# A modulation sum moved from VectorE to ScalarE and GpSimd, and one copy of B for the scan states

## The chip, the core and the metric

The kernel runs on one core of a Trainium2 chip. The core has TensorE (matmuls, PE in the profile, with the weight loads as PEld), VectorE (DVE), ScalarE (ACT), GpSimd (POOL) and SyncE (SP), which here only issues the transfers. Each engine executes its own instruction queue in order, and they wait for one another by semaphores. The metric is the device time of one execution in microseconds; the times here are the median of several runs.

## What is computed

Two layers of a diffusion backbone over 512 latent tokens of width 1024, with 256 context tokens. A conditioning vector gives each layer six modulation vectors:

```python
mod = (silu(c) @ ada_w[i] + ada_b[i])[:, None, :]
sh1, sc1, g1, sh2, sc2, g2 = jnp.split(mod, N_MOD, axis=-1)      # parts 0 to 5
hx = modulate(rms_norm(x, norm_mix[i]), sh1, sc1)
# layer 0: attention (8 heads) beside a bidirectional scan, both from one input projection
m_lat, _ = hybrid_mixer(hx, hc, ...)       # layer 1: shortconv_mixer(hx, ...)
x = x + g1 * m_lat
x = x + g2 * swiglu(modulate(rms_norm(x, norm_ffn[i]), sh2, sc2), w_gate, w_up, w_down)
```

The scan works in chunks of 128 tokens: two of context, four latent ones. For each chunk, direction and group it forms a state, a product of B (128 tokens x 64) and the decayed inputs (128 tokens x 256):

```python
states = einsum('bclgn,bgecl,bclgep->bcgepn', bc, decay_to_end, xdt)
h = h * chunk_decay + states        # forward over the chunks, and backward for the other direction
```

## The kernel before

Everything is kept with features on the partitions, in float32. A large matmul is made of three of reduced type: each operand is split into a high part (a cast on ScalarE, L94) and a rest (a subtraction on VectorE, L95), and `mm3` (L114 to L118) adds high x high, high x rest and rest x high. Weights come through one ring of three staging buffers named `wst` (512 KB each, L107) and are split into rings of `whi` and `wlo`, also three each.

Layer 0's mixer (`mixer`, L388) first projects keys, values, queries and six feature tiles. It then runs three Python generators round by round (L497 to L505). `ssd` (L695) makes features 6 to 9, advances the scan's states, and then does eight `ssd_unit`s, one per chunk and group (L740). `attention` (L846) does eight heads in two rounds each, and prepares the row maxima of a later head (`attn_prep`, L787, its maximum on VectorE at L804, its diagonal matrix on ScalarE at L805) while it runs the scores and exponentials of the present one (`attn_head`, L811, exponentials at L824). The third is `ada_rest` (L236).

`ada_rest` computes modulation parts as a weighted sum over the 1024 rows of `ada_w`. Per half part (512 columns) it loads four pieces of 2 x 128 rows into `wst` (L251). The first slice is multiplied by its column of silu(c) on VectorE (L255), and the other seven are multiplied and added there (L257, one operation each, two full operands and a per-partition scalar). A 32x32 block transpose (L260) and a reduction (L261) leave 16 numbers per partition in `red`. When all parts are done, one small matmul (L264) folds the partitions, and L269 adds the bias. In the mixer it is called for layer 0's parts 2, 3 and 4: the gate of the mixer, needed at L916 in the projection that follows, and the shift and scale of the first FFN, needed in `entry` (L937) behind that. Its accumulator and its transposed copy lie in `xtok`, in the two context chunks. It is pumped two steps per round from the seventh round on. The parts of layer 1 and part 5 are summed in the same way during the first FFN, with an accumulator `ada_acc`.

The states: `to_tok` (L578) transposes feature 4, which holds B, and copies it for each chunk to `btok` twice side by side, once for each direction, six copies on ScalarE (L590). `ssd_states` (L645) multiplies the inputs by the decay on GpSimd (L652) and takes the matmul with the doubled B (L656), so its output has 128 partitions, of which the forward direction uses the lower and the backward one the upper 64. For the context both directions come from one matmul of 512 columns per chunk and group. For the latent chunks `advance` (L704) does one direction and chunk after the other, with one matmul of 256 columns per group, each with its own PSUM bank. `ssd_advance` (L663) scales the old state on GpSimd (L673) and adds the new one on VectorE (L676). PSUM has three banks of kind A, one of kind V and two double ones of kind S.

The order of the instructions on each engine isn't the program's: a planner takes, in a modelled run, for each engine the earliest instruction in program order that is ready. An instruction that comes late in the program but has its data early fills gaps. Only where the program says so (`manual_schedule`) an engine keeps the program's order. What the planner wrote is fixed, so an engine waits for an instruction in front although a later one may be ready.

## Time and profile before

| | us |
|---|---|
| median of three runs (1287.85 to 1292.81) | 1289.33 |
| the profiled execution | 1291.26 |
| its span in the trace | 1289.4 |
| TensorE busy | 1239.6 (96%) |
| VectorE busy | 729.4 (57%) |
| ScalarE busy | 448.4 (35%) |
| GpSimd busy | 179.5 (14%) |

The shares are averages over stages with different limits. About 1.9 us of the profiled execution lie around its span. Matmuls are pipelined and their ends are modelled, so busy times of TensorE overlap and a busy TensorE is not one at its peak. The stretch around the change, with the context states, the attention, the scan and the modulation sum, goes from about 130 to 326 us.

### The profile page before, as it was taken

To read this page: it belongs to the slowest core of one execution; us is meant where nothing else is said; L and a number is where in the kernel's file an instruction comes from. 1 tells how busy PE (TensorE), PEld (TensorE's weight loads), DVE (VectorE), ACT (ScalarE), POOL (GpSimd) and SP (SyncE) were. 2 spreads that over 40 slices of the span, in tenths; PEclk is the share of its full clock that TensorE was granted. 3 is DMA by queue.
4 is the path that set the end of the run, shared out by engine and by line. 5 is a ranking of instruction groups with operands and counts; after the bars stand their busy time and mean duration, and the time that the engine had idled before them with its cause. 6 is when DMAs were issued, how large, how long until landed. Compare 5 with 4: busy or idle time off the path is not lost.

```text
span 1289.4 us, 15875 instructions
## 1 busy us (share of the span) xinstructions
PE 1239.6 (96%) x6086; PEld 1021.6 (79%) x6086; DVE 729.4 (57%) x1187; ACT 448.4 (35%) x675; POOL 179.5 (14%) x199
## 2 busy tenths in 40 slices
PE   5998988899999999999999999999999999999997
PEld 3887765567898888888888988888988888888886
DVE  4898799985564777788422554443743333332223
ACT  3534534455353222223222342223532222222221
POOL 3423335440220000000000100002200000000001
PEclk9999989999999999999999999999999999999998
DMA  9331343300514777777333323333133333333322
GB/s 369 127 99 49 96 155 125 115 17 1 163 50 143 227 243 243 235 240 249 118 91 94 111 79 93 95 97 112 50 114 98 99 98 98 97 91 90 94 87 66
DMA packets 54845, 158.52 MB, mean 123 GB/s; under 512 B 6000, under 2 KB 8688, under 8 KB 54512
## 3 DMA queue, kind: packets, MB, share of 16 engines
q1 hardware_dynamic: 54480, 157.20, 38.1%
q8 instruction: 48, 0.79, 0.2%
q10 hardware_dynamic: 288, 0.31, 0.1%
q14 instruction: 29, 0.24, 0.1%
HBM read 154.86 MB, written 2.10 MB: 122 GB/s over the span
## 4 chain that ended last, share of the span: by engine, by line
PE 83%; DVE 9%; DMA 3%; issue 3%; POOL 1%; ACT 0%; SPq 0%; DVEq 0%; ACTq 0%; POOLq 0%
PE psS L116 14%; PE psS L117 14%; PE psS L118 14%; PE psA L116 10%; PE psA L118 10%; PE psA L117 10%; DVE xtok L257 2%; PE psV L830 2%; DMA adaw<-ada 2%; PE psS L961 1%; PE psS L822 1%; DVE mx L804 1%; DVE wlo L95 1%; PE psS L963 1%; DMA xT<-xT 1%
## 5 line engine op out<-in xcount | busy, mean ns | idle before, releaser
L95 DVE TENSOR_TENSOR wlo<-wst,whi 128x1024 fp32r<-128x1024 f32 (+2 forms) x194 | 235.0, 1214 | 315.2 <-ACT whi L94 312.3
L94 ACT CAST whi<-wst 128x1024 fp32r<-128x1024 f32 (+2 forms) x194 | 198.2, 1025 | 544.8 <-PE psS L117 242.1
L116 PE MATMUL psS<-act_hi,whi 128*128 128x512 f32 x760 | 297.0, 391 | 1.2 <-DVE cs_a L573 1.0
L117 PE MATMUL psS<-act_lo,whi 128*128 128x512 f32 x760 | 296.7, 390 | 0.0
L118 PE MATMUL psS<-act_hi,wlo 128*128 128x512 f32 x760 | 296.6, 390 | 0.0
L118 PEld LDWEIGHTS psS<-act_hi,wlo 128*128 128x128 f32 x760 | 143.1, 188 | 29.7
L116 PEld LDWEIGHTS psS<-act_hi,whi 128*128 128x128 f32 x760 | 143.0, 188 | 29.5 <-issue 1.2
L117 PEld LDWEIGHTS psS<-act_lo,whi 128*128 128x128 f32 x760 | 143.0, 188 | 27.9
L325 POOL TENSOR_TENSOR sq_acc<-sq_acc,sq 128x512 f32<-128x512 f32 (+1 forms) x28 | 38.0, 1356 | 872.5 <-issue 645.8
L116 PE MATMUL psA<-ffn_h_hi,whi 128*128 128x512 f32 (+1 forms) x396 | 145.3, 367 | 0.0
L118 PE MATMUL psA<-ffn_h_hi,wlo 128*128 128x512 f32 (+1 forms) x396 | 144.9, 366 | 0.0
L117 PE MATMUL psA<-ffn_h_lo,whi 128*128 128x512 f32 (+1 forms) x396 | 144.8, 366 | 0.0
L257 DVE SCALAR_TENSOR_TENSOR ada_acc<-ada_st,silu_c,ada_acc 128x512 f32<-128x512 f32 x98 | 73.4, 749 | 27.5 <-DMA ada_st<-ada 26.0
L117 PEld LDWEIGHTS psA<-ffn_h_lo,whi 128*128 128x128 f32 x396 | 74.7, 189 | 12.1
L116 PEld LDWEIGHTS psA<-ffn_h_hi,whi 128*128 128x128 f32 x396 | 74.7, 189 | 12.0
L118 PEld LDWEIGHTS psA<-ffn_h_hi,wlo 128*128 128x128 f32 x396 | 74.7, 189 | 12.0
L116 PE MATMUL psA<-act_hi,whi 128*128 128x512 f32 (+1 forms) x216 | 80.0, 370 | 0.0
L118 PE MATMUL psA<-act_hi,wlo 128*128 128x512 f32 (+1 forms) x216 | 79.2, 367 | 0.8 <-DVE wlo L95 0.8
L117 PE MATMUL psA<-act_lo,whi 128*128 128x512 f32 (+1 forms) x216 | 79.5, 368 | 0.0
L916 DVE SCALAR_TENSOR_TENSOR xT<-psA,mod,xT 128x512 f32<-128x512 f32 (+1 forms) x40 | 25.7, 643 | 68.2 <-PE psA L118 68.0
L94 ACT CAST ffn_h_hi<-sg 128x512 fp32r<-128x512 f32 x44 | 27.4, 622 | 59.1 <-DVE sg L980 59.1
L118 PEld LDWEIGHTS psA<-act_hi,wlo 128*128 128x128 f32 x216 | 40.8, 189 | 8.0 <-DVE wlo L95 1.3
(297 smaller groups left out, 1804.4 us busy)
## 6 DMA issues: line engine op xcount, KB each, us to landing
wst<-w_gu SPq DMA_DIRECT2D x88, 512.0 KB, 3.6
ada_st<-ada SPq DMA_DIRECT2D x112, 256.0 KB, 4.0
wst<-w_dn SPq DMA_DIRECT2D x32, 512.0 KB, 3.5
wst<-ada SPq DMA_DIRECT2D x24, 512.0 KB, 3.8
wst<-w_sc SPq DMA_DIRECT2D x24, 512.0 KB, 3.6
adaw<-ada SPq DMA_DIRECT2D x16, 512.0 KB, 10.4
wst<-w_dn SPq DMA_DIRECT2D x16, 384.0 KB, 3.2
wst<-w_f SPq DMA_DIRECT2D x10, 512.0 KB, 3.6
```

The lines of the kernel that those rows point to most:

```text
L94: nc.scalar.copy(hi, src)
L95: nc.vector.tensor_tensor(lo, src, hi.bitcast(F32), ALU.subtract)
L116: nc.tensor.matmul(out, lhsT=a[0], rhs=b[0], start=start, stop=False)
L117: nc.tensor.matmul(out, lhsT=a[0], rhs=b[1], start=False, stop=False)
L118: nc.tensor.matmul(out, lhsT=a[1], rhs=b[0], start=False, stop=stop)
L257: nc.vector.scalar_tensor_tensor(a, w[:, i], c, a, ALU.mult, ALU.add)
L325: nc.gpsimd.tensor_tensor(self.acc[:, ts], self.acc[:, ts], sq, ALU.add)
L804: nc.vector.tensor_reduce(mx[:, c:c + 1], s[:, 0:768], AX.X, ALU.max)
L822: nc.tensor.matmul(s[:, a * T:a * T + T], lhsT=kt[x][:, ks], rhs=q[x], start=(x == 0), stop=(x == 1))
L830: nc.tensor.matmul(av, lhsT=vz[:, kc, vs], rhs=e[:, a], start=(c + a == 0), stop=(c + a == CHUNKS - 1))
L916: nc.vector.scalar_tensor_tensor(xt[:, d, ts], ps, gate[:, d:d + 1], xt[:, d, ts], ALU.mult, ALU.add)
L961: nc.tensor.matmul(out, lhsT=a[:, k * P:(k + 1) * P], rhs=hi, start=(k == 0 and a is w[0]), stop=False)
```

## The change

Three things are changed.

1. The modulation sum of layer 0's mixer is split. Part 2 stays as it was on VectorE, pumped one step per round from the seventh round. Parts 3 and 4 get a generator of their own, pumped one step per round from the second round. It multiplies each slice by its column in place on ScalarE and adds the slices on GpSimd into a new accumulator `ada_more`. Transposes and reductions stay on VectorE, into other columns of `red`; there are now two folds.
2. B is kept once in `btok`: two copies instead of six.
3. `ssd_states` takes pairs of chunk and direction. Each has a matmul of 64 output rows and 256 columns, forward into the lower and backward into the upper 64 partitions of one bank, the two behind each other in fixed order. `advance` makes both states first and then both advances.

```diff
-    def ada_rest(self, pool, layer, parts, acc=None, bufs=2, tag=None):
+    def ada_rest(self, pool, layer, parts, acc=None, bufs=2, tag=None, pair=False, red=0):
...
                         c = self.sc[:, 0, k + i:k + i + 1]
-                        if k + i == 0:
+                        if pair:
+                            nc.scalar.activation(w[:, i], w[:, i], AF.Copy, scale=c)
+                            if k + i:
+                                nc.gpsimd.tensor_tensor(a, w[:, 0] if k + i == 1 else a, w[:, i], ALU.add)
+                        elif k + i == 0:
                             nc.vector.tensor_scalar(a, w[:, i], c, None, ALU.mult)
                         else:
                             nc.vector.scalar_tensor_tensor(a, w[:, i], c, a, ALU.mult, ALU.add)
...
-                nc.vector.tensor_reduce(self.red[:, 2 * n + j], tr.rearrange("p (b i) -> p b i", i=32), AX.X, ALU.add)
+                nc.vector.tensor_reduce(self.red[:, red + 2 * n + j], tr.rearrange("p (b i) -> p b i", i=32), AX.X, ALU.add)
...
-        nc.tensor.matmul(ps, lhsT=self.con("fold"), rhs=self.red[:, 0:2 * np_], start=True, stop=True)
+        nc.tensor.matmul(ps, lhsT=self.con("fold"), rhs=self.red[:, red:red + 2 * np_], start=True, stop=True)
...
-        btok = sm.tile([P, CHUNKS, 2, 2, 64], F32, name="btok")
+        btok = sm.tile([P, CHUNKS, 2, 64], F32, name="btok")
...
-        ada = [self.ada_rest(None, 0, (2, 3, 4), (xtok[:, 0], xtok[:, 1]))]
+        more = mp.tile([P, T], F32, name="ada_more")
+        ada = [self.ada_rest(None, 0, (2,), (xtok[:, 0], xtok[:, 1]))]
+        other = [self.ada_rest(None, 0, (3, 4), (more, xtok[:, 1]), pair=True, red=4)]
...
             alive = (next(a, 1) is None) or alive
+            if rounds > 0:
+                self.pump(1, other)
             if rounds > 5:
-                self.pump(2, ada)
+                self.pump(1, ada)
             rounds += 1
         self.pump(1000, ada)
+        self.pump(1000, other)
...
-            s = tp.rearrange("p c (g n) -> p c g n", g=2)
-            for c in range(nc_):
-                nc.scalar.copy(btok[:, c0 + c], s[:, c, :, None, :].broadcast_to([P, 2, 2, 64]))
+            nc.scalar.copy(btok[:, c0:c0 + nc_], tp.rearrange("p c (g n) -> p c g n", g=2))
...
-    def ssd_states(self, sp, sd, c, dirs, tag):
+    def ssd_states(self, sp, sd, ends, tag):
...
-            st = self.psA()
-            for e in dirs:
+            st = self.psA((P, 256))
+            for c, e in ends:
                 nc.gpsimd.tensor_tensor(
...
-            lo, n = 256 * dirs[0], 256 * len(dirs)
-            nc.tensor.matmul(st[:, lo:lo + n], lhsT=sd["btok"][:, c, g].rearrange("p a b -> p (a b)"),
-                             rhs=xw.rearrange("p a b c -> p (a b c)")[:, lo:lo + n], start=True, stop=True)
-            for e in dirs:
-                r = slice(64 * e, 64 * e + 64)
-                out.append((g, e, st[r, 256 * e:256 * e + 256]))
+            with self.tc.manual_schedule(engines={mybir.EngineType.PE}):
+                for c, e in ends:
+                    nc.tensor.matmul(st[64 * e:64 * e + 64], lhsT=sd["btok"][:, c, g], rhs=xw[:, e], start=True, stop=True)
+                    out.append((g, e, st[64 * e:64 * e + 64]))
...
-        st0 = self.ssd_states(pp, sd, 0, (0, 1), "cs_a512")
+        st0 = self.ssd_states(pp, sd, ((0, 0), (0, 1)), "cs_a512")
...
-        st1 = self.ssd_states(pp, sd, 1, (0, 1), "cs_a512")
+        st1 = self.ssd_states(pp, sd, ((1, 0), (1, 1)), "cs_a512")
...
         def advance(a, b):
+            st = self.ssd_states(sp, sd, ((2 + a, 0), (2 + b, 1)), "da")
             for f, t, e in ((a, a + 1, 0), (b, b - 1, 1)):
-                self.ssd_advance(sd, hin[t], hin[f], self.ssd_states(sp, sd, 2 + f, (e,), "da"), 2 + f, e)
+                self.ssd_advance(sd, hin[t], hin[f], st, 2 + f, e)
```

## Rows read from the trace of the kernel before

**Rows 1.** Stages: us, busy PE, PEld, DVE, ACT, POOL, granted clock, DMA share, GB/s:

```profile
160.00:180.00 20.00, 16.21 (x56) 11.52 (x56) 17.78 (x27) 6.94 (x12) 8.42 (x13) 0.83 0.45 148
220.00:240.00 20.00, 17.19 (x61) 11.10 (x60) 18.51 (x31) 9.12 (x15) 10.48 (x9) 0.91 0.33 103
270.00:290.00 20.00, 18.91 (x76) 12.89 (x75) 15.00 (x28) 10.03 (x16) 8.50 (x8) 1.00 0.00 1
290.00:326.00 36.00, 36.00 (x164) 26.14 (x163) 19.03 (x41) 18.41 (x29) 0.00 (x0) 1.00 0.00 1
150.00:270.00 120.00, 105.24 (x397) 71.78 (x396) 113.36 (x179) 49.69 (x82) 56.84 (x58) 0.96 0.38 119
193.00:284.00 91.00, 80.89 (x300) 52.48 (x299) 83.85 (x139) 43.03 (x72) 47.22 (x40) 0.98 0.30 92
```

**Rows 2.** Waits of TensorE, 150 to 290 us: total us, times, longest:

```profile
PE psS L802 <- DVE mx L804: 3.2, 3, 1.3
PE psS L751 <- DVE mx L804: 2.9, 2, 1.7
PE psS L822 <- DVE mx L804: 2.3, 1, 2.3
PE psS L751 <- ACT ex L824: 2.0, 2, 1.2
PE psA L779 <- DVE lx L774: 1.5, 2, 1.4
PE psA L808 <- ACT dm L805: 1.5, 1, 1.5
PE psA L656 <- DVE zf L479: 0.9, 1, 0.9
```

**Rows 3.** Chain of waits, 186 to 230 us, shares by line:

```profile
by line: DVE xtok L257 23.7%; DVE mx L804 10.9%; PE psV L830 7.8%; PE psS L822 6.5%; issue 6.2%; DVE ada_red L261 4.5%; DVE xtok L255 4.4%; PE psS L802 3.9%; DVE xtok L260 3.3%; DVE lx L774 3.3%; PE psA L758 2.6%; DVE hin L676 2.5%; DVE lx
```

**Rows 4.** VectorE's groups, 150 to 270 us: count, busy us, mean ns, idle before:

```profile
L257 DVE SCALAR_TENSOR_TENSOR xtok<-wst,silu_c,xtok 128x512 f32<-128x512 f32 x42 | 36.3, 865 | 2.7 <-DMA wst<-ada 2.2
...
L255 DVE TENSOR_SCALAR xtok<-wst,silu_c 128x512 f32<-128x512 f32 x6 | 4.9, 824 | 0.9 <-DMA wst<-ada 0.9
L260 DVE STREAM_TRANSPOSE xtok<-xtok 128x512 f32<-128x512 f32 x6 | 4.2, 700 | 0.1
...
L261 DVE TENSOR_REDUCE ada_red<-xtok 128x16 f32<-128x512 f32 x6 | 4.0, 674 | 0.1
```

**Rows 5.** Timeline of VectorE at 313 us: start, us, operation:

```profile
313.04 0.76 DVE L269 TENSOR_TENSOR mod<-psA,vecs 32x24 f32<-32x24 f32 x4 [0.33 <-PE psA L264]
```

**Rows 6.** ScalarE's groups, 750 to 870 us:

```profile
L1026 ACT ACTIVATE sc_a<-sc_g,vecs 128x512 f32<-128x512 f32 x8 | 5.8, 723 | 0.0
```

**Rows 7.** GpSimd's groups, whole span:

```profile
L325 POOL TENSOR_TENSOR sq_acc<-sq_acc,sq 128x512 f32<-128x512 f32 x20 | 30.6, 1532 | 851.8 <-issue 645.8 <-ACT sq L322 205.9
```

**Rows 8.** Timeline of GpSimd at 338 us:

```profile
338.15 3.84 POOL L325 TENSOR_TENSOR sq_acc<-sq_acc,sq 128x512 f32<-128x512 f32 x2 [53.21 <-ACT sq L322]
```

**Rows 9.** Timeline of VectorE at 201 us:

```profile
201.37 2.93 DVE L257 SCALAR_TENSOR_TENSOR xtok<-wst,silu_c,xtok 128x512 f32<-128x512 f32 x2
```

**Rows 10.** Timeline of GpSimd at 201 us:

```profile
201.26 1.04 POOL L755 TENSOR_TENSOR da<-cons,dta_hi 128x512 fp32r<-128x512 f32 x1 [0.96 <-PE psA L758]
202.26 1.49 POOL L755 TENSOR_TENSOR da<-cons,dta_lo 128x512 fp32r<-128x512 f32 x1
203.71 1.48 POOL L770 TENSOR_TENSOR lx<-lx,dt 128x512 f32<-128x512 f32 x1
```

**Rows 11.** The page's group of the same sum in the first FFN:

```profile
L257 DVE SCALAR_TENSOR_TENSOR ada_acc<-ada_st,silu_c,ada_acc 128x512 f32<-128x512 f32 x98 | 73.4, 749 | 27.5 <-DMA ada_st<-ada 26.0
```

**Rows 12.** TensorE's groups, 140 to 326 us, the states:

```profile
L656 PE MATMUL psA<-xw,btok 128*128 128x256 f32 x24 | 7.6, 430 | 0.9 <-DVE zf L479 0.9
...
L656 PE MATMUL psA<-xw,btok 128*128 128x512 f32 x8 | 4.5, 641 | 2.2 <-POOL xw L652 1.1 <-ACT btok L590 1.1
```

**Rows 13.** Timeline of TensorE at 34 us:

```profile
34.37 1.07 PE L203 MATMUL psS<-adaw,silu_w 128*32 128x256 f32 x16 [1.08 <-issue]
```

## The prediction

> **What bounds the kernel now.** I read the stage table first, because the busy shares of the whole span hide the place: the change works between about 130 and 326 us, where the context states, the attention and the scan run. From 290 us on TensorE is busy without a gap (36.00 of 36.00 us), and nothing off TensorE can be worth time there [rows 1]. From 150 to 270 us it is different: VectorE is busy 113.36 of 120.00 us (94.5%), TensorE 105.24, ScalarE 49.69 and GpSimd 56.84 [rows 1]. So TensorE stands idle 14.8 us there, 12.3%. The stretch 270 to 290 us does the same kind of work without the modulation sums on VectorE: VectorE 15.00 of 20.00 us (75%), TensorE idle 1.09 us (5.5%) [rows 1].
>
> Next the waits of TensorE, which say who is late. Of its nine rows between 150 and 290 us the seven longest stand: VectorE ends 3.2 + 2.9 + 2.3 + 1.5 + 0.9 = 10.8 us of them, ScalarE 2.0 + 1.5 = 3.5 us, GpSimd none [rows 2]. Most of VectorE's are the row maximum L804, which frees a score bank of PSUM; it is late because it stands in VectorE's queue behind other work. The chain of waits says which work: from 186 to 230 us L257, L261, L255 and L260, all of the modulation sum, hold 23.7 + 4.5 + 4.4 + 3.3 = 35.9% of the chain, some 15.8 of 44 us [rows 3]. The idle time costs twice: the granted clock is 0.83 in 160 to 180 us and 0.91 in 220 to 240 us, so a part of both stretches ran at 1.2 instead of 2.4 GHz, while TensorE waited for 3.8 of the first 20 us and 2.8 of the second [rows 1]. At full clock that is (1 - 0.83) x 20 + (1 - 0.91) x 20 = 5.2 us.
>
> **What leaves VectorE.** Six half parts cost 42 L257 of 865 ns, 6 L255 of 824, 6 transposes of 700 and 6 reductions of 674 [rows 4]. Parts 3 and 4 are four of the six. Their 28 L257 and 4 L255 go: 28 x 0.865 + 4 x 0.824 = 27.5 us. Their transposes and reductions stay, and a second fold with its four small additions L269 adds about 0.8 us (four of 24 elements took 0.76 us) [rows 5]; the fold's own matmul is of the same small kind. In the rows of before the fold's result came at 313 us, long after the last sum; it has to be there only for the gate of the projection and the entry of the FFN behind it, so I put no price on its time.
>
> **What comes to ScalarE and GpSimd.** 32 products (eight per half part). The same form, Copy with a scale vector, 128x512, takes 723 ns at L1026 [rows 6]: 23.1 us. Then 7 sums per half part, 28 in all, of two full 128x512 operands. The nearest row is the sum of squares L325, 1532 ns on average; two in a row took 3.84 us, 1.92 each [rows 7, 8]. That is 42.9 us, with 53.8 us as the upper end.
>
> **What of it is given back: the collision.** The traces show VectorE and GpSimd slowing each other. At 201.37 us two L257 take 2.93 us together, while GpSimd runs three operations back to back, of which the second and third take 1.49 and 1.48 us after 1.04 for the first [rows 9, 10]. In the first FFN the same L257 averages 749 ns over 98 [rows 11]; taken as its unhindered length, one collision costs VectorE about 0.72 us. If none of the 28 sums meets such an operation it is nothing, if all do, 20 us; I take half, 10.1 us, since two thirds of the operations exposed to it (the L257) leave, while the scan's own stay. VectorE's relief is then 27.5 - 0.8 - 10.1 = 16.6 us, and its load in 150 to 270 us 96.8 of 120, or 81%.
>
> One rule speaks against the change. The Trainium skill (SBUF — State Buffer, section "SBUF: two separate sides") says that the port pair that VectorE and GpSimd share is an exclusive lock, held for a whole instruction, with the loser fully blocked. The trace agrees only in part: three GpSimd operations and two L257 would have needed 3 x 1.04 + 2 x 0.75 = 4.6 us one after the other and took 3.9 [rows 9, 10]. What full blocking would make of the time is the second rival.
>
> **What that is worth on TensorE.** Between 81% load and the two states that I have, 94.5% with 12.3% idle and 75% with 5.5%, a straight line gives 7.6% idle, 9.1 us instead of 14.8: 5.7 us won. The upper end is all that VectorE ends, 10.8 us. I take 8, since the sums are not spread evenly over VectorE's work but sit on the chain [rows 3]. Of the 5.2 us of low clock I take half, 2.6 (ends 0 and 5.2).
>
> **The states.** Before, 12 products of 256 columns and 4 of 512, each in two instructions, took 7.6 + 4.5 = 12.1 us of TensorE's (overlapping) busy time [rows 12]; half of each output was thrown away for the context. Now 20 products of 64 output rows and 256 columns, in pairs that lie in different column halves of the array. The row for such halves is the start's L203: 16 instructions with 32 output rows and 256 columns in 1.07 us [rows 13]. That is 0.067 us each, where a full-width row of 256 columns has 430 ns with overlap [rows 12]. So the pairs gain something between nothing and half, and up to 4 us; I take 2 us on the path, as part of TensorE's time there is covered by waits. Half as many PSUM banks per advance help GpSimd, on which nobody waits. Two copies of B instead of six end the 1.1 us that TensorE waits for it [rows 12]: 0.6 us.
>
> **What the new work costs on the path.** (a) ScalarE goes from 49.7 to about 73 of 120 us, 41% to 61%. Behind a product stand the exponentials L824 and L767 and the diagonal L805, for which TensorE waits. Scaling TensorE's 3.5 us of such waits by the load gives 5.2, so 1.7 us (ends 0 and 5). (b) The wait for the 16 loads of parts 3 and 4 moves from VectorE's queue to ScalarE's. VectorE waited 2.2 + 0.9 = 3.1 us for 24 [rows 4], so 2.1 us, of which half counts: 1.0. Those loads also stand in SyncE's queue ahead of two output weights, which nobody needs before the projection. (c) GpSimd's own queue: behind a sum stand the decay operands L755 and the scaling L770, which feed TensorE and VectorE. Of 28 sums, some nine should fall among the scan's units, and delay an operand by less than their length: 2.0 us (ends 0 and 28 x 1.53 = 43). (d) The four transposes wait for the last sum of a half part, with L804 behind them, and the next half part's first sum waits for the transpose, as there is one accumulator: 1.0 us (ends 0 and four times 1.9). Together 5.7 us.
>
> **The sum.** Gains 8.0 + 2.6 + 2.0 + 0.6 = 13.2, costs 5.7, net 7.5 us. The profiled execution took 1291.26 us, so 1283.8; it lies 1.93 us above the median of the runs, so the forecast is 1281.8 us.
>
> **Rivals.** *The sums hold VectorE* (no change). Every sum meets an operation that reads two operands, and 20.2 us of the 26.7 come back. VectorE's load stays at (113.4 - 6.5) / 120 = 89%, idle time on the line at 10.4%, 2.3 us won, and 2.6 for states and copies; costs 5.7, net +0.8 us: 1290 us. For it: GpSimd gets a long operation per 128x512 slice. Against it: the 42 L257 average 865 ns although GpSimd is busy 57 of 120 us [rows 1, 4], so before only a few collided.
>
> *Every sum blocks VectorE for its whole length* (slower). Where each of the 28 sums stops VectorE for 1.53 us instead of 0.72, 42.9 us come against the 26.7 that leave, and the 16.2 us of difference lengthen a stretch that VectorE already fills: nothing won there, 2.6 for states and copies, costs 5.7, so 1291.3 + 16.2 - 2.6 + 5.7 = 1310.6, on the median 1309 us. Against it: three operations and two L257 took less than their sum [rows 9, 10]. This is what the rule of the Trainium skill named above (SBUF — State Buffer, section "SBUF: two separate sides") would do here if every sum met an exposed operation.
>
> *GpSimd becomes the bound* (slower). From 193 to 284 us the eight units run, 91 us, with 47.2 us of GpSimd [rows 1]. If all sums fell there at 1.92 us, 47.2 + 53.8 = 101 us: 10 us more than there is. The context's gain of 2.6 stays, VectorE's is gone: 1291.3 + 10.0 - 2.6 = 1298.7, on the median 1297 us. It decides from (91 - 47.2) / 1.92 = 23 sums in that stretch. For it: the loads share three buffers with the weights, and are late if these hold them. Against it: the new sums start a round after the first feature, and GpSimd has long idle time before 193 us (8.42 busy of 20 in 160 to 180) [rows 1].
>
> *VectorE was the whole limit* (more gain). All 10.8 us and the full 5.2 of clock come back, states give 4, and the costs hide: 1291.3 - 10.8 - 5.2 - 4 - 0.6 + 2 = 1272.7, on the median 1271 us.
>
> **How the numbers follow.** Forecast 0.50 (1276 to 1287 us), VectorE held 0.24, whole blocking 0.03, GpSimd bound 0.09, whole limit 0.14. The time given is the forecast's. The range 1271 to 1291 us leaves out the two slower cases and about half of the last. A measurement tells about 0.5% from no change: 1282.9 and 1295.8 us. Faster takes all of the last case and 0.38 of the forecast, 0.52; same the rest of the forecast and VectorE held, 0.36; slower the blocking and the GpSimd case, 0.12.
>
> **What would show it.** Right: VectorE in 150 to 270 us falls to about 80%, L257 is x14 there, TensorE's waits for L804 shrink to a third, the granted clock stays above 0.95 in 160 to 180 us, and the units end some 7 us earlier, with the kernel behind 330 us as long as before. Wrong: L773, L774 and L757 rows that grow by GpSimd's length; waits of TensorE for L755; transposes L260 waiting for GpSimd; or an idle time of TensorE that stays although VectorE is free, which would mean that the attention's own chain set the pace.

## The result, and the profile after

The changed kernel takes 1303.7 us (median of four runs, 1301.5 to 1304.8) against 1290.5 us for the kernel before (median of four). The ratio is 1.0097, with a 95% interval from 1.0075 to 1.0118: slower by 13 us, where 7.5 us of gain were forecast. The profiled execution took 1301.5 us, with a span of 1299.7; it is the fastest of the four.

The stages, in the columns of [rows 1]: time, busy PE, PEld, DVE, ACT and POOL with their counts, granted clock, DMA share, GB/s.

```profile
160.00:180.00 20.00, 16.01 (x68) 10.77 (x67) 15.06 (x21) 10.57 (x18) 14.24 (x18) 0.91 0.50 159
220.00:240.00 20.00, 15.18 (x44) 9.78 (x44) 19.63 (x26) 10.56 (x16) 18.60 (x14) 0.83 0.38 113
290.00:326.00 36.00, 34.91 (x164) 25.77 (x165) 27.05 (x59) 22.25 (x36) 1.04 (x2) 1.00 0.00 1
150.00:270.00 120.00, 100.79 (x362) 65.12 (x363) 89.42 (x132) 61.73 (x102) 87.64 (x82) 0.91 0.36 114
193.00:284.00 91.00, 78.36 (x273) 50.09 (x273) 73.13 (x115) 47.79 (x78) 60.99 (x49) 0.93 0.28 88
```

From 150 to 270 us VectorE fell from 113.36 to 89.42 us, to 75% (forecast 81%). TensorE did not gain by it: it is idle 19.2 us instead of 14.8, and its granted clock fell from 0.96 to 0.91. GpSimd rose from 56.84 to 87.64 us. From 220 to 240 us VectorE is still busy 19.63 of 20 us, and the clock is 0.83 there.

TensorE's waits between 150 and 290 us, in the columns of [rows 2] (L829, L786, L815, L809 were L822, L779, L808, L802; the maximum L811 was L804):

```profile
PE psS L829 <- DVE mx L811: 4.5, 4, 2.4
PE psA L786 <- DVE lx L781: 3.7, 2, 2.9
PE psA L815 <- ACT dm L812: 3.3, 1, 3.3
PE psS L809 <- DVE mx L811: 2.9, 1, 2.9
```

The waits for the row maximum, 3.2 + 2.9 + 2.3 = 8.4 us before, are 4.5 + 2.9 = 7.4; a third was forecast. The wait for L781, the last step of the scan's decay matrix on VectorE, went from 1.5 to 3.7 us.

The groups of the new work on ScalarE and GpSimd, and of the scan's multiply-add on VectorE, from 150 to 270 us: count, busy us, mean ns, idle time before with its cause.

```profile
L255 ACT ACTIVATE wst<-wst,silu_c 128x512 f32<-128x512 f32 x28 | 18.8, 715 | 16.9 <-DMA wst<-ada 15.3 <-issue 1.7
L257 POOL TENSOR_TENSOR ada_more<-ada_more,wst 128x512 f32<-128x512 f32 x23 | 32.8, 1426 | 5.3 <-ACT wst L255 2.8 <-issue 1.6
L780 DVE SCALAR_TENSOR_TENSOR lx<-lx,dt 128x128 f32<-128x128 f32 x20 | 10.7, 593 | 0.0
```

The multiply-add in the kernel before, in the same stretch:

```profile
L773 DVE SCALAR_TENSOR_TENSOR lx<-lx,dt 128x128 f32<-128x128 f32 x24 | 8.4, 408 | 0.0
```

Product and sum cost what was forecast (715 ns for 723, 1426 for 1532). What was not forecast is the multiply-add, 593 ns instead of 408; the prediction named its growth (L773) as a sign of being wrong. Four L780 in a row take 1.13 us where GpSimd leaves them alone (at 245.71 us in this trace); that is 0.28 us each. Here is one such group with what follows it, and GpSimd beside it (start, length, instruction, count):

```profile
230.49 4.60 DVE L780 SCALAR_TENSOR_TENSOR lx<-lx,dt 128x128 f32<-128x128 f32 x4
235.01 0.68 DVE L894 TENSOR_TENSOR ao<-ao,as 128x512 f32<-128x512 f32 x1
235.61 0.68 DVE L781 TENSOR_TENSOR lx<-lx,cbs 128x512 f32<-128x512 f32 x1
236.21 2.06 DVE L95 TENSOR_TENSOR wlo<-wst,whi 128x1024 fp32r<-128x1024 f32 x1
238.19 1.76 DVE L95 TENSOR_TENSOR act_lo<-ao,act_hi 128x512 fp32r<-128x512 f32 x1
239.87 0.94 DVE L811 TENSOR_REDUCE mx<-psS 128x1 f32<-128x768 f32 x1
```

```profile
227.06 4.44 POOL L257 TENSOR_TENSOR ada_more<-ada_more,wst 128x512 f32<-128x512 f32 x3
231.57 1.04 POOL L762 TENSOR_TENSOR da<-cons,dta_hi 128x512 fp32r<-128x512 f32 x1
232.57 1.09 POOL L762 TENSOR_TENSOR da<-cons,dta_lo 128x512 fp32r<-128x512 f32 x1
233.62 1.31 POOL L257 TENSOR_TENSOR ada_more<-ada_more,wst 128x512 f32<-128x512 f32 x1
235.68 1.51 POOL L762 TENSOR_TENSOR da<-cons,dta_hi 128x512 fp32r<-128x512 f32 x1 [0.74 <-PE psA L765]
237.15 2.25 POOL L257 TENSOR_TENSOR ada_more<-ada_more,wst 128x512 f32<-128x512 f32 x1
```

GpSimd runs without a gap from 227.06 to 234.93 us. The four short instructions end one by one at 231.65, 232.76, 233.81 and 235.08 us, each 0.15 us behind the end of one of its four operations (231.50, 232.61, 233.66 and 234.93): 4.60 us instead of 1.13. At 234.93 GpSimd stops for 0.74 us, and the next two VectorE instructions take their normal 0.68 us; the second began 0.07 us ahead of GpSimd's next operation, and now that one is the longer, 1.51 instead of 1.04 us. Then VectorE loses again: `wlo` takes 2.06 us (1.27 on average before, from 140 to 330 us), `act_lo` 1.76 instead of 0.68. The maximum, for which TensorE has been waiting 2.9 us, stands behind all of them.

These rows lie in the head of attention that grows most. Counted from the last cast that a head's queries need (L809, now L816) to the next head's, the heads before start at 188.0, 206.7, 234.6 and 255.4 us, after at 191.0, 212.4, 245.8 and 266.0. So the one stretch of 27.9 us became 33.5, and VectorE is full in it in both kernels. The two profiled spans differ by 10.3 us: 5.6 arise in this head and 5.7 ahead of it, which are not traced here; some 1 us is won back later. The head before, then after (the second window is 0.5 us wider than the head):

```profile
206.70:234.60 27.90, 23.94 (x84) 15.16 (x83) 27.62 (x49) 11.90 (x21) 12.27 (x10) 0.94 0.30 95
```

```profile
212.00:246.00 34.00, 25.31 (x82) 16.60 (x81) 32.84 (x45) 17.77 (x29) 26.42 (x19) 0.85 0.43 137
```

The multiply-adds in the second window, as a group:

```profile
L780 DVE SCALAR_TENSOR_TENSOR lx<-lx,dt 128x128 f32<-128x128 f32 x10 | 7.9, 843 | 0.0
```

VectorE needs 32.84 us there for 45 instructions, where it needed 27.62 for 49. Against their undisturbed lengths, its ten L780 lost 7.9 - 10 x 0.28 = 5.1 us, `wlo` and `act_lo` some 0.8 + 1.1, four L261 4.5 - 4 x 0.75 = 1.5 (with the 749 ns of [rows 11]), and a copy 1.5 - 0.4 = 1.1: together 9.6 us. In the same head before, the multiply-adds and ten L257 had lost 4.9 - 12 x 0.28 = 1.5 and 8.8 - 10 x 0.75 = 1.3 us.

The chain of waits through this head says the same. Before, its largest pieces are TensorE's; after, the multiply-add holds 21.4% of 33.4 us, 7.1 us, where it held 3.7% of 27.9, 1.0 us. The chain before, then after:

```profile
by line: PE psV L830 19.4%; PE psS L822 11.0%; DVE xtok L257 9.3%; DVE mx L804 7.1%; PE psS L802 6.1%; DVE lx L774 5.2%; PE psA L758 4.1%; ACT ex L824 3.7%; DVE lx L773 3.7%; issue 3.4%; PE psS L757 3.3%; PE psA L761 3.0%; DVE xf L784 2.5%;
```

```profile
by line: DVE lx L780 21.4%; DMA wst<-ada 11.8%; DVE xtok L261 11.2%; PE psA L786 6.1%; DVE wlo L95 5.9%; DVE mx L811 5.6%; issue 5.2%; PE psA L787 5.2%; DVE act_lo L95 5.0%; DVE rt L892 4.5%; DVE xf L791 3.9%; DVE lx L781 3.8%; DVE xtok L26
```

The next in the second chain are late loads (DMA wst<-ada) and part 2's sum (L261), which waits for them.

### The profile page after: what moved, and what is told of

Same layout as the page of the kernel before. It is cut to its first block, busy times and chain, and to the rows that moved or that the text cites. A ratio compares the mean times of both kernels' runs of the same rounds, so it can differ in the third digit from the quotient of the medians.

```text
span 1299.7 us, 15929 instructions
## 1 busy us (share of the span) xinstructions
PE 1243.1 (96%) x6096; PEld 1020.6 (79%) x6096; DVE 715.8 (55%) x1159; ACT 468.1 (36%) x703; POOL 217.2 (17%) x227
## 4 chain that ended last, share of the span: by engine, by line
PE 81%; DVE 7%; DMA 6%; issue 3%; ACT 1%; POOL 1%; SPq 0%; DVEq 0%; ACTq 0%; POOLq 0%
PE psS L117 13%; PE psS L116 13%; PE psS L118 13%; PE psA L116 10%; PE psA L118 10%; PE psA L117 10%; PE psV L837 2%; DMA wst<-ada 2%; DMA ada_st<-ada 2%; DMA adaw<-ada 2%; DVE wlo L95 2%; PE psS L968 1%; PE psS L829 1%; PE psS L970 1%; DVE xtok L261 1%
## 5 line engine op out<-in xcount | busy, mean ns | idle before, releaser
L95 DVE TENSOR_TENSOR wlo<-wst,whi 128x1024 fp32r<-128x1024 f32 (+2 forms) x194 | 238.2, 1231 | 316.0 <-ACT whi L94 311.2
L261 DVE SCALAR_TENSOR_TENSOR ada_acc<-ada_st,silu_c,ada_acc 128x512 f32<-128x512 f32 x98 | 73.5, 750 | 28.9 <-DMA ada_st<-ada 27.3
L117 PEld LDWEIGHTS psA<-ffn_h_lo,whi 128*128 128x128 f32 x396 | 74.7, 189 | 12.1
L837 PE MATMUL psV<-ex,vz 128*128 128x512 f32 x96 | 47.5, 619 | 0.0
```

What stands on the lines that cost most here:

```text
L95: nc.vector.tensor_tensor(lo, src, hi.bitcast(F32), ALU.subtract)
L117: nc.tensor.matmul(out, lhsT=a[0], rhs=b[1], start=False, stop=False)
L261: nc.vector.scalar_tensor_tensor(a, w[:, i], c, a, ALU.mult, ALU.add)
L837: nc.tensor.matmul(av, lhsT=vz[:, kc, vs], rhs=e[:, a], start=(c + a == 0), stop=(c + a == CHUNKS - 1))
```

## The experiments

Two questions were open after the result: which part costs the 13 us, and where the gain of a lighter VectorE went. All times are medians, and ratios are to the kernel before, run beside them (1290.7 to 1292.3 us). The 95% interval of a ratio reaches 0.10 to 0.29% to either side, 1.3 to 3.7 us.

**The parts of the change alone.** The states and the single B, with the modulation sum as before:

```diff
-        other = [self.ada_rest(None, 0, (3, 4), (more, xtok[:, 1]), pair=True, red=4)]
+        ada = [self.ada_rest(None, 0, (2, 3, 4), (xtok[:, 0], xtok[:, 1]))]
...
-                self.pump(1, ada)
+                self.pump(2, ada)
...
```

> Only parts 2 and 3 of the change: B once, states in pairs; the modulation sum stays whole on VectorE as before. By the prediction's terms for states and copies this is 2.6 us faster than the kernel before, 1287 to 1288 us, with ends 1284 and 1290. Rival (the states are what makes the changed kernel slower, since they form both states ahead of both advances and the planner's order moves): 1300 us or more. If the modulation sum alone is to blame, this kernel stays within 3 us of before.

1292.4 us, ratio 1.0006 (0.9994 to 1.0018): nothing. The 40 matmuls have 8.5 us of busy time where [rows 12] had 12.1, and the idle time before them fell from 3.0 to 2.3 us, but the end does not show it.

The changed kernel without the 32 products, all 28 sums kept:

```diff
-                            nc.scalar.activation(w[:, i], w[:, i], AF.Copy, scale=c)
```

> The changed kernel with the 28 sums on GpSimd, but without the 32 products on ScalarE (raw rows are summed, parts 3 and 4 wrong); the loads are then awaited by GpSimd. Theory A (ScalarE's queue): it falls to within 4 us of the kernel without both. Theory B (GpSimd's sums): it stays near the changed kernel, 1300 to 1304 us, and the scaling L780 still averages about 500 ns instead of 391.

1301.7 us, 1.0081 (1.0064 to 1.0099), the multiply-add at 504 ns over all 32: the loss is still there. Next, the products kept and only the first of seven sums per half part:

```diff
-                            if k + i:
+                            if k + i == 1:
```

> The changed kernel with the 32 products on ScalarE, but 4 instead of 28 sums on GpSimd (parts 3 and 4 wrong). Theory A (ScalarE's products wait for their loads at the head of its queue, 16.2 us in the trace, and exponentials and diagonals stand behind them): the time stays near the changed kernel, 1300 to 1304 us. Theory B (GpSimd's sums collide with VectorE's two-operand operations and delay the decay operands): it falls to within 4 us of the kernel without both.

1289.6 us, 0.9987 (0.9977 to 0.9998): the loss is gone, with ScalarE at 67.87 of 120 us. So it is GpSimd's sums. The products cost nothing here (1289.6 us also without them, in loads_only below); beside the sums it may be up to 2.0 us (1303.7 against 1301.7, with intervals that overlap). The same from the other side, with the sums on VectorE behind the products on ScalarE:

```diff
-                                nc.gpsimd.tensor_tensor(a, w[:, 0] if k + i == 1 else a, w[:, i], ALU.add)
+                                nc.vector.tensor_tensor(a, w[:, 0] if k + i == 1 else a, w[:, i], ALU.add)
```

> The changed kernel with its 28 sums on VectorE instead of GpSimd; the products stay on ScalarE. VectorE has the same number of long instructions as in the kernel before. If GpSimd's sums are the whole loss and ScalarE's products cost nothing: 1289 to 1293 us. If the products or the split of the sum over two engines cost by themselves once VectorE is full: 1295 us or more.

1292.2 us, 1.0014 (0.9999 to 1.0029), with VectorE back at 108.36 of 120 us.

**Is it GpSimd's time or its reading?** 24 of the 28 sums are replaced by memsets, which hold GpSimd and the buffers but read nothing:

```diff
-                            if k + i:
-                                nc.gpsimd.tensor_tensor(a, w[:, 0] if k + i == 1 else a, w[:, i], ALU.add)
+                            if k + i == 1:
+                                nc.gpsimd.tensor_tensor(a, w[:, 0], w[:, i], ALU.add)
+                            elif i == 1:
+                                for _ in range(3):
+                                    nc.gpsimd.memset(w, 0.0)
```

> The changed kernel with its products, but 24 of the 28 GpSimd sums are replaced: per pair of products three GpSimd memsets of 1024 columns on the same buffer, so that GpSimd is held about as long and the buffers are released as late, but it reads nothing from SBUF. Parts 3 and 4 are therefore not computed. If the sums cost by making VectorE's two-operand instructions wait for a whole GpSimd read: 1289 to 1292 us, the scan's multiply-add on 128x128 back at about 0.34 to 0.40 us. If they cost by filling GpSimd's queue ahead of the scan's own operands: 1299 to 1304 us as in the changed kernel, with GpSimd's busy time between 150 and 270 us at 80 us or more.

1289.0 us, 0.9993 (0.9980 to 1.0007): 14.6 us less than the changed kernel (13.4 by the ratios). The memsets on GpSimd from 140 to 340 us, and the stage from 150 to 270:

```profile
L260 POOL MEMSET wst<- 128x1024 f32 x36 | 33.6, 952 | 7.3 <-ACT wst L255 7.0
```

```profile
150.00:270.00 120.00, 106.71 (x399) 70.07 (x400) 95.02 (x148) 66.56 (x110) 89.98 (x98) 0.94 0.36 114
```

GpSimd is busy 89.98 us, even more than with the sums (87.64), and TensorE is back at 106.71. The head that took 33.5 us takes 26.9. That is 6.6 of the 10.6 us between the two profiled spans (1299.7 and 1289.1). The engines in that head, the group of its multiply-adds (843 ns with the sums) and its chain of waits:

```profile
208.60:235.60 27.00, 22.94 (x82) 14.88 (x80) 25.11 (x42) 16.72 (x29) 19.63 (x19) 0.87 0.39 125
```

```profile
L783 DVE SCALAR_TENSOR_TENSOR lx<-lx,dt 128x128 f32<-128x128 f32 x12 | 4.2, 404 | 0.0
```

```profile
by line: PE psV L840 10.0%; ACT wst L255 9.1%; DVE rt L895 8.0%; issue 7.5%; DVE lx L783 6.8%; DVE ce L778 6.3%; DVE xtok L264 5.8%; PE psS L767 5.0%; PE psS L761 4.5%; DVE xf L794 4.5%; DVE mx L814 3.7%; DVE lx L784 2.6%; DVE ao L897 2.6%;
```

The multiply-add's share of the chain is down from 7.1 us to 6.8% of 26.9, 1.8 us. So GpSimd's queue is not the cost; that its sums read from SBUF beside VectorE is, as far as memsets can stand in for them. This is what the Trainium skill states (SBUF — State Buffer, section "Who interferes with whom"): a VectorE instruction with two SBUF inputs contends with a GpSimd instruction that reads SBUF, not with one that only writes. One difference remains: memsets have no order through an accumulator, sums have. And over all 32 the multiply-add averages 415 ns with the memsets, a little above the 0.34 to 0.40 us expected and not far below the changed kernel's 499; it is in the one head that the two kernels differ by a factor of two.

**Shorter GpSimd instructions.** Each sum is cut into two of 256 columns:

```diff
-                                nc.gpsimd.tensor_tensor(a, w[:, 0] if k + i == 1 else a, w[:, i], ALU.add)
+                                for h in (slice(0, 256), slice(256, 512)):
+                                    nc.gpsimd.tensor_tensor(a[:, h], w[:, 0, h] if k + i == 1 else a[:, h], w[:, i, h], ALU.add)
```

> The changed kernel with each GpSimd sum cut into two of 256 columns (56 instead of 28; 256-column sums take 0.74 to 0.80 us elsewhere in this kernel, so GpSimd has a little more to do). If an exposed VectorE instruction waits for one whole GpSimd instruction, it now waits half as long for each sum it meets, and about half of the 14.7 us comes back: 1293 to 1298 us. If GpSimd's total time (its queue ahead of the scan's operands) is what costs: 1301 to 1306 us.

1300.9 us, 1.0060 (1.0038 to 1.0081). The mean of the scan's multiply-add fell from 499 to 415 ns over all 32, as it should; but that is also its mean with the memsets, at 1289.0 us, so this mean does not follow the time. And a half takes more than half a sum:

```profile
L258 POOL TENSOR_TENSOR ada_more<-ada_more,wst 128x256 f32<-128x256 f32 x48 | 39.8, 849 | 6.1 <-ACT wst L255 4.9 <-ACT cbs L771 0.8
```

Two halves are 1.70 us for 1.42, and GpSimd comes to 96.92 of 120 us. Some 3 to 5 us came back (by the medians 2.8, by the ratios 0.4%), not the 6 to 11 expected. In the profiled execution the costly head takes 32.0 us for 33.5, and starts 3.1 us later (215.5 us). How far that is GpSimd's longer time and how far something else is open.

**What a lighter VectorE is worth.** The kernel before without parts 3 and 4 at all, with constants in their place:

```diff
+        nc.vector.memset(self.mod, 1.0)
...
+        nc.vector.memset(self.gsc, 1.0)
...
-        ada = [self.ada_rest(None, 0, (2, 3, 4), (xtok[:, 0], xtok[:, 1]))]
+        ada = [self.ada_rest(None, 0, (2,), (xtok[:, 0], xtok[:, 1]))]
```

> The kernel before without parts 3 and 4 of the modulation sum: neither their loads nor their 28 + 4 VectorE instructions, four transposes and four reductions; the scale and shift of the FFN are constants. This is the relief that the change was made for, without any of its costs. The prediction's own step (VectorE relieved, 14.8 us of TensorE's idle time between 150 and 270 us fall by 8, clock 2.6): 1290.5 - 10.6 = 1280 us, VectorE's load at about 69%. The rival, that attention's own chain of dependences sets TensorE's idle time and VectorE's load does not: 1287 to 1290 us, with TensorE's busy time in 150 to 270 us still at 104 to 107.

1279.3 us, 0.9913 (0.9898 to 0.9928): 11.7 us of gain, where the forecast's two steps together said 10.6. Without part 2 as well (`ada = []`):

> The kernel before without parts 2, 3 and 4: no modulation sum during attention and scan at all, and none of the 24 loads; gate, shift and scale are constants. If VectorE's load is the limit, all 10.8 us of TensorE's waits for VectorE and 5.2 us of clock come back: 1274 us. If attention's own chain is the limit: 1285 to 1289 us, with TensorE still idle for 9 us or more between 150 and 270 us and its longest waits still those for the row maximum.

1276.3 us, 0.9888 (0.9873 to 0.9903). So the forecast's figure fits parts 3 and 4 as a whole, work and loads together. But the changed kernel without its products and 24 of its sums, which leaves VectorE as light as that, gives almost none of it (its loads stay):

```diff
-                            nc.scalar.activation(w[:, i], w[:, i], AF.Copy, scale=c)
-                            if k + i:
+                            if k + i == 1:
```

> The changed kernel without the 32 products on ScalarE and with 4 instead of 28 sums on GpSimd (parts 3 and 4 are therefore wrong); the loads, transposes and reductions stay. This is the relief of VectorE without the work that took its place. The prediction's step from VectorE's load to TensorE's idle time says 8 + 2.6 + 2.6 = 13 us faster than before, 1276 us. Rival (the stretch is paced by TensorE and its own chain, VectorE's load was busy time that mattered little): no more than 4 us faster, 1286 us or above. Either way it tells what the products and sums together cost: changed kernel minus this one.

1289.6 us, 0.9991 (0.9981 to 1.0001). The stage from 150 to 270 us, in this kernel and then without parts 3 and 4:

```profile
150.00:270.00 120.00, 105.51 (x402) 69.20 (x403) 91.50 (x146) 49.90 (x82) 58.81 (x62) 0.96 0.34 112
```

```profile
150.00:270.00 120.00, 112.27 (x442) 78.42 (x441) 93.96 (x156) 56.01 (x93) 59.54 (x63) 0.99 0.16 49
```

VectorE is busy 91.50 against 93.96 us, and TensorE 105.51 against 112.27. What differs most is the DMA, 112 against 49 GB/s. Waits of loads_only from 150 to 270 us, three of VectorE's rows and two of SyncE's, and TensorE's longest:

```profile
DVE wlo L95 <- ACT whi L94: 5.9, 2, 3.0
DVE xtok L260 <- DMA wst<-ada: 4.6, 2, 3.2
DVE xtok L263 <- POOL ada_more L256: 2.5, 1, 2.5
```

```profile
SPq L251 <- DMA wst<-ada: 38.4, 12, 5.0
SPq L251 <- POOL ada_more L256: 5.8, 3, 2.7
```

```profile
PE psS L828 <- DVE mx L810: 7.0, 3, 4.4
```

VectorE is not full, but it stands in order in front of instructions whose loads are late. The row maximum stands behind them: TensorE's waits for it are 7.0 + 2.0 + 1.8 = 10.8 us from 150 to 290 us. To see whether it is the loads, the changed kernel without loads and products, and with 4 sums of a cleared tile (transposes, reductions and fold stay):

```diff
-                        w = halves(self.wp.tile([P, 1024], F32, name="wst", tag="wst", bufs=3))
-                    nc.sync.dma_start(out=w, in_=t["ada"][layer, part * 2 + j, :, k:k + step, :])
+                        w = None if pair else halves(self.wp.tile([P, 1024], F32, name="wst", tag="wst", bufs=3))
+                    if not pair:
+                        nc.sync.dma_start(out=w, in_=t["ada"][layer, part * 2 + j, :, k:k + step, :])
...
+                            if k + i == 1:
+                                nc.gpsimd.tensor_tensor(a, a, a, ALU.add)
```

> The changed kernel without the 16 loads, the 32 products and 24 of the 28 sums of parts 3 and 4 (4 sums add a cleared tile to itself); the four transposes, four reductions and the second fold stay. Beside loads_only (1289.6 us) it lacks only the loads; beside no_34 (1279.3 us) it adds the small rest. If the loads, through the three buffers and SyncE's queue that they share with the weights, eat the relief: 1279 to 1283 us, and VectorE's waits for DMA and for the weight halves (13 us in loads_only with the wait for the sum) under 5. If the transposes and the second stream of steps eat it: 1287 to 1290 us.

1281.3 us, 0.9917 (0.9897 to 0.9938). The 16 loads with their turns of the buffers are 8.3 us (9.5 by the ratios), and TensorE's waits for the maximum are down to 5.2 us (3.6 + 1.6). With loads of 64 instead of 512 columns in the same buffers and order:

```diff
+                    n0 = 64 if pair else 512
+                    nc.sync.dma_start(out=w[:, :, 0:n0], in_=t["ada"][layer, part * 2 + j, :, k:k + step, 0:n0])
...
+                            if k + i == 1:
+                                nc.gpsimd.tensor_tensor(a, a, a, ALU.add)
+                                nc.gpsimd.tensor_tensor(a[:, 0:64], w[:, 0, 0:64], w[:, 1, 0:64], ALU.add)
...
```

> The changed kernel with 16 loads of an eighth of the size (64 of 512 columns, 64 KB instead of 512 KB) into the same buffers in the same order, without products and with 4 (and 4 short) sums: parts 3 and 4 are not computed. Beside loads_only (1289.6 us) and no_load (1281.3 us). If the time that a load's bytes take (4.7 us to landing, 2.3 us a load at the rate reached) is what holds the buffers and SyncE's queue: 1281 to 1284 us. If it is the buffers' turn itself (three buffers, each taken and released in order by five readers): 1287 to 1290 us.

1283.2 us, 0.9945 (0.9924 to 0.9965): some six of them are the time that the bytes take. The rest, 1.9 us by the medians and 3.6 by the ratios, is the turn of the buffers, with four short sums. And the fourth field of the table, VectorE's work without the loads:

```diff
+                        w = halves(self.wp.tile([P, 1024], F32, name="wst", tag="wst", bufs=3)) if part == 2 else None
...
+                        wi = a if w is None else w[:, i]
...
-                            nc.vector.scalar_tensor_tensor(a, w[:, i], c, a, ALU.mult, ALU.add)
+                            nc.vector.scalar_tensor_tensor(a, wi, c, a, ALU.mult, ALU.add)
```

> The kernel before with VectorE's 28 + 4 instructions of parts 3 and 4 kept, but on the accumulator itself instead of loaded data: its 16 loads are gone, so parts 3 and 4 are not computed. It fills the fourth field of a table: work and loads 1290.5 us, loads without work 1289.6, neither 1279.3 to 1281.3. If VectorE's load and the loads are two limits of about the same height, of which either alone holds the time: 1287 to 1291 us, VectorE at 92% or more between 150 and 270 us. If the loads alone were the limit: 1280 to 1284 us although VectorE is as full as before.

1294.2 us, 1.0023 (1.0010 to 1.0036), VectorE at 113.44 of 120 us as before: 3 us above its expected range, so the loads are not the limit alone. So:

| parts 3 and 4 | loads | no loads |
|---|---|---|
| VectorE's sums | 1290.5 to 1292.3 (before) | 1294.2 |
| none | 1289.6 | 1281.3 |

Either of the two holds the time by itself. Taking away one gives nothing, or 1 us, as long as the other stands. Why the kernel without the loads is even 0.23% slower than the one before is open.

**The sums without the loads.** As no_load, with all 28 sums:

```diff
-                            if k + i == 1:
+                            if k + i:
```

> As no_load, but with all 28 GpSimd sums (of a cleared tile with itself), so the sums come without loads and products. If the price of the sums (changed kernel less memsets: 1303.7 - 1289.0 = 14.7 us) is their reading against VectorE's two-operand instructions, it comes whatever the loads do: some 12 to 16 us above no_load, 1292 to 1299 us. If it needs the late loads (a sum that waits and holds the rest up): under 5 us above no_load.

1288.3 us, 0.9974 (0.9963 to 0.9984): 7 us above no_load, between what the two theories said. The collision does not need the loads, but half of its price went with them. Not by the loads' time alone: without a load to wait for, the sums also run earlier, the last at 212.31 us instead of 237.15, so that one falls into the head that cost the most, where the changed kernel has eight. And without the loads the move itself pays: GpSimd's sums 1288.3 us, VectorE's 1294.2 (the products, without a price in few_sums, are missing in the first).

**The same work later.** In the kernel before, parts 3 and 4 start in round 10 or 14, one step a round, the rest behind the last round:

```diff
-        ada = [self.ada_rest(None, 0, (2, 3, 4), (xtok[:, 0], xtok[:, 1]))]
+        ada = [self.ada_rest(None, 0, (2,), (xtok[:, 0], xtok[:, 1]))]
+        other = [self.ada_rest(None, 0, (3, 4), (xtok[:, 0], xtok[:, 1]))]
...
+            if rounds >= 14:
+                self.pump(1, other)
...
```

> The kernel before with all its sums on VectorE, but parts 3 and 4 begin only in round 10 of 19 and take one step a round instead of two; eight of their 16 steps stand behind the last round. If what hurts is VectorE and the loads between 190 and 250 us, while VectorE is free for 17 us of the 36 behind 290 us: 1280 to 1286 us. If the delayed sums land on the path behind the scan (the output projection starts late): 1290 to 1300 us.

> As late_10, but from round 14 of 19: 4 of 16 steps in the rounds, 12 behind the last one. If the time from 190 to 290 us is what counts, the same heads' pace as without parts 3 and 4 (about 20 us a head from 203 us on) and 1279 to 1285 us; if 28 long VectorE instructions and 8 MB of loads do not fit behind 280 us, the output projection waits for its weights or for VectorE: 1288 to 1300 us.

1291.3 and 1291.4 us, 0.9999 (0.9986 to 1.0013) and 1.0003 (0.9989 to 1.0016). These two moved only half of what they were made to move. The planner put the sums of part 3 into gaps ahead of 212 us all the same: some 27 or 28 of the 42 L257 run before that time in both kernels, as in the kernel before, and part 2 has only 14. Part 4 alone came later. Up to 247 us late_14 runs the heads nearly as without parts 3 and 4 (the head that starts at 246.7 us starts at 244.3 there), and then loses it again, with the sums of part 4 between 263 and 294 us. The sums L257 of late_14 by stretches, each with busy time and count of these instructions alone, granted clock, DMA share and GB/s:

```profile
150.00:170.00 20.00, 5.50 (x7) 0.91 0.43 136
170.00:190.00 20.00, 8.54 (x11) 1.00 0.46 150
190.00:210.00 20.00, 8.68 (x10) 1.00 0.50 155
250.00:270.00 20.00, 2.31 (x4) 1.00 0.15 42
270.00:290.00 20.00, 6.76 (x8) 0.91 0.35 110
290.00:330.00 40.00, 2.24 (x3) 1.00 0.20 63
```

From 270 to 290 us VectorE is then busy 19.66 of 20 us, and whether part 4's sums or their loads hold the time there was not separated. The changed kernel with its steps in rounds 14 to 17, or 12 to 16 (four or three a round):

```diff
-            if rounds > 0:
-                self.pump(1, other)
+            if rounds >= 14:
+                self.pump(4, other)
```

> The changed kernel with parts 3 and 4 moved behind the scan's units: their 16 steps in rounds 14 to 17 of 19, four a round, where GpSimd has nothing else. If the price of the change is the collision of the sums with the scan's multiply-adds and of the loads with part 2's and the scan's order: the first five heads at no_34's pace, little VectorE work left to collide with, 1281 to 1287 us. If the products and sums, which cannot run faster than the loads (16 times 2.3 us = 37 us), hold ScalarE's exponentials of the last two heads: 1290 to 1300 us.

> As gp_14, but three steps a round from round 12. The loads have five rounds instead of four; about six of 28 sums still meet the last units. If pace of the loads is what costs in gp_14: faster than gp_14 by 2 to 6 us, 1282 to 1288 us. If meeting the units costs: slower than gp_14 by 2 to 4 us.

1301.6 us, 1.0084 (1.0055 to 1.0113), and 1300.5 us, 1.0072 (1.0050 to 1.0095). These two do not test what they were made for either. The planner moved the sums forward into gaps of GpSimd's order, among the units, where the multiply-adds now average 717 and 719 ns over all 32; the sums of gp_14 by stretches:

```profile
190.00:210.00 20.00, 12.19 (x10) 1.00 0.49 157
210.00:230.00 20.00, 5.66 (x5) 1.00 0.17 54
230.00:250.00 20.00, 9.32 (x7) 0.91 0.25 79
250.00:270.00 20.00, 8.34 (x7) 1.00 0.26 79
```

Whether sums behind the units would be free wasn't tried: it would need an order by hand. No version that computes everything was faster than the kernel before.

## Why the prediction was wrong

**What was right.** The count and the length of the new instructions, and that VectorE's work holds the stretch: with that work and without the loads it is as slow as before (work_no_load). Attention's own chain, named as a sign of failure, is not the limit, since no_234 gains 14.8 us. The worth of VectorE's relief, 8 + 2.6 = 10.6 us, lies near the 11.7 of no_34, but that is luck: no_34 lacks the loads too, and the forecast gave their absence no worth.

**First failed step: "What that is worth on TensorE".** It read the worth off the line between two states of VectorE's load, and put it to the change's credit. But at the low end of the line (270 to 290 us, [rows 1]) not only the sums are missing; the loads are, too (DMA share 0.00 there, 0.38 in the stretch). The line is that of no_34, not of the change. With the loads left in, the 10.6 us are 1.1 us (loads_only, 0.9981 to 1.0001), or 9.5 us too many in the sum. That the loads wait in turn behind three buffers stood at nothing there, but for the 1.0 us of step (b). VectorE's waits for loads in [rows 4], 2.2 + 0.9 = 3.1 us, gave no warning: an engine that is busy 113.36 of 120 us has little time in which to wait.

**Second failed step: "the collision".** The term priced a collision at 0.72 us per sum and let half of the 28 sums meet one: 10.1 us of VectorE's time, taken out of its average load. Measured, the sums cost 14.6 us at the end (changed kernel against memsets; 13.4 by the ratios). The rows show a price that goes by VectorE's instructions, not by the sums: four short ones of 0.28 us each waited for the end of an operation of GpSimd, and took 4.60. The argument that "two thirds of the operations exposed to it (the L257) leave" counted only the long ones; the scan's L773 (L780), little over a third as long, pay more for their size. And these stay on the path of the scan, with the maximum behind them: VectorE's average fell to 75%, but in the head that grows most it is 32.84 of 34 us. Of the end's loss, 5.6 us were followed to that head (6.6 against the memsets); for the rest the rows were not followed.

**The rival that came nearest** is "every sum blocks VectorE for its whole length", given 0.03 and 1309 us. That a sum blocks for its whole length is what the rows show; the sum made of it is not. It put 16.2 us more work on VectorE, whose busy time fell by 23.9 us from 150 to 270 us. That its time was only 5 us too long is in part luck. Against it stood [rows 9, 10], where three GpSimd operations and two L257 took 3.9 us and not the 4.6 of strict turns; that row is of two long instructions, and says nothing of four short ones. "GpSimd becomes the bound" was refuted by memsets (GpSimd 89.98 of 120 us, 1289.0 us).

**The smaller steps.** The states' 2.0 and the copies' 0.6 us are nothing (states_only). Steps (a) and (b), 2.7 us for ScalarE's queue and its loads, are 0.0 us without the sums (few_sums against loads_only), and 2.0 by the medians with them (changed kernel against no_products, with intervals that overlap). Step (c), 2.0 us for GpSimd's queue with some nine sums among the units: 14 sums fell there (193 to 240 us), and TensorE's waits for the decay operands rose to 1.3 us only, with one of 3.5 us for the states' operand L660 ahead of 150 us (1.1 before). Step (d), 1.0 us for transposes behind sums: VectorE's waits of the changed kernel have no such row. So the sum, in the order of the forecast: gains 1.1 instead of 13.2, costs 14.6 instead of 5.7; that is 13.5 us slower, where 13.1 were measured. It is no independent check, since memsets and loads_only, the two runs that it goes by, lie within 0.6 us of each other; that they do says that products and GpSimd's time come to nothing.

## What to carry to other kernels

When an engine is 95% busy, look for what is second in line before you price its relief: here the loads of the moved work held the same stretch, and the work taken away without them was worth 1.1 us, where both together were worth 11.7. A sum on GpSimd is not free because GpSimd is idle: count the short VectorE instructions with two SBUF operands that will run beside it, each of which can pay a whole GpSimd operation. An average of an engine's load over a stage hides that it may be full in the one part that sets the time.

## What the hardware showed

- Four VectorE multiply-adds of 128x128 took 4.60 us beside GpSimd's two-operand operations and 1.13 us without; each ended 0.15 us behind one of GpSimd's operations of 1.04 to 1.31 us. This agrees with the lock held for a whole instruction (the Trainium skill, SBUF — State Buffer, section "SBUF: two separate sides").
- GpSimd's memsets of 1024 columns (952 ns each), which brought it to 89.98 of 120 us, cost the kernel nothing: 1289.0 us, and 1289.6 without them (few_sums).
- One GpSimd sum of 128x512 took 1.42 us on average beside VectorE's work, two of 128x256 took 1.70 (half_sums).
- Matmuls of 64 output rows in pairs of column halves took 8.5 us of busy time for 40 (states_only) where 32 full-width ones took 12.1, without moving the end of the kernel.
